# Gate and up products with both parts of the activations in one matmul of 512 columns

## The chip, the cores and the metric

One core of a Trainium2 chip runs one program. The metric is the device time of one execution in microseconds (us). Most executions of a kernel agree within 0.3%. The kernel must give float32 results close to those of the reference, which is why every large product is made from operands cut into two parts.

## The reference

Two blocks work on x [256 tokens, 1024 features] in float32. The first has two layers, each of a gated feed-forward block, three mixers side by side (a recurrence over 6 heads, dilated attention, a gated convolution) with an input and an output projection, and a second gated feed-forward block:

```
_swiglu(x, w_gate, w_up, w_down) = (silu(x @ w_gate) * (x @ w_up)) @ w_down
x = x + 0.5 * _swiglu(_rms_norm(x, norm_ffn1[l]), ...)
x = x + mix @ w_out[l]
x = x + 0.5 * _swiglu(_rms_norm(x, norm_ffn2[l]), ...)
```

The second block has one layer: attention, a short convolution and windowed means side by side, and a feed-forward block in which gate and up pass a convolution of three taps over the tokens before silu(gate) * up. There are thus five feed-forward blocks, each with 2816 hidden units, that is 22 hidden tiles of 128.

## The kernel before

**Layout.** Features lie on partitions and tokens along the free dimension: a tile of x is [128 features, 256 tokens], and there are 8 of them (ND). A hidden tile is [128 hidden units, 256 tokens].

**Two parts.** Every large operand a is cut into a high part (rounded to float32r) and a low part (what is left). A product is three matmuls: high by high, high by low, low by high; the product of the two low parts is left out. `piece` (line 258) loads a [128, 1024] piece of weights into a raw tile (3 of these), makes the high part on ScalarE (line 271, 6 tiles) and the low part on VectorE (line 272, 5 tiles). In the last feed-forward block the down weights are also freed of their rows' mean (lines 266 to 269). `hilo` (line 322) and `split` (line 394) make the two parts of activations, in two tiles xh and xl. `mm3` (line 278) issues the three matmuls; the weight block is the stationary operand and is loaded anew before each, the activations stream through, 256 columns. All records of matmuls stand on line 276, in `mm`.

**One feed-forward block** (`ffn`, line 414). For each of the 22 hidden tiles: three pieces (gate, up, down); 8 x 2 weight blocks of gate and up products, alternating between gate and up, into one bank of PSUM named rk, gate in its first half and up in its second (lines 427 to 431); the gate step (line 446, or line 1136 in the last block); the two parts hh and hl of the hidden tile (lines 434 to 437); then the 8 down products of the hidden tile before, into four banks that stay for the whole block (two named mm, two named at; lines 438 to 440). So a hidden tile's down products follow the gate and up products of the next one. The last three hidden tiles are kept: their down products come at the end, output tile by output tile (`ends`, line 405): for five output tiles those of the first two kept hidden tiles, then, output tile by output tile, those of the last hidden tile, each followed by the residual and the next norm.

The very first hidden tile (`fresh`) takes all gate products before the up products; its weights arrive with x.

**Gate steps.** `swiglu` multiplies both halves of the bank by the norm's factor R in one VectorE instruction (line 448), then silu on ScalarE (450) and a product on VectorE (452). `conv_gate` takes each half by a ScalarE instruction with scale and bias (line 1141) and two taps on VectorE (1142, 1143), and between hidden tiles one step of the next norm's work on the residual (lines 1073 and 1083).

**What sets the order.** The framework's scheduler puts the instructions of each engine in order by priority and by a model of their times, and gives out the tiles; each engine then works through its queue in that order. In the trace VectorE casts weight pieces between the steps of the gate. The eight banks of PSUM are named mm (3), rk (2) and at (3); `accs` (line 391) takes two mm and two at.

**Other users of the parts.** `colsB` (line 325) and `colsA` (line 332) make the input projections; in `colsA` the activations are the stationary operand and the weights stream with up to 512 columns. `w_out` (line 951) makes the output projections, `Norm.tile` (line 357) and `LayerNorm.end` (line 1098) cut x for the products that follow.

Of the kernel before, what the change touches and what calls it, by code (L numbers as in the profile page):

```python
# [21 lines left out]
FIRST = 2 * 3 * ND + 128      # of the small arrays: the gains of the norms, and the identity  # L22
# [4 lines left out]
KO = (0, 2, 4, 6, 1, 3, 5, 7)      # so that neighbours lie in different banks of PSUM  # L27
EXPH = math.exp(-0.5)
ALPHA = 2.0 ** 0.25
NEG = -1e30  # L30


# ---------------------------------------------------------------- host side: layout, and constants of the shapes
class Pack:
    """small arrays side by side in one [128, n] array"""
# [17 lines left out]
def _pt(v):  # L53
    """[n*128] -> [128, n]"""
    return v.reshape(-1, 128).T


def _ffn_pack(g, u, d):
    """[22*128, 3072]: for each tile of 128 hidden units its gate columns, up columns, down rows"""
    out = np.empty((NF, 128, 3, 1024), np.float32)  # L60
    out[:, :, 0] = g.reshape(8, 128, NF, 128).transpose(2, 1, 0, 3).reshape(NF, 128, 1024)
    out[:, :, 1] = u.reshape(8, 128, NF, 128).transpose(2, 1, 0, 3).reshape(NF, 128, 1024)
    out[:, :, 2] = d.reshape(NF, 128, 1024)
    return out.reshape(NF * 128, 3072)


def _cols(w, c0, n):
    """columns c0..c0+n of w [K, *] -> [128, K/128 * n]"""
# [99 lines left out]
# ---------------------------------------------------------------- the kernel  # L168
@with_exitstack
def tile_model(ctx, tc, A, at, out):  # L170
# [55 lines left out]
    # ---- constants  # L226
# [30 lines left out]
    # ---- weights: a piece is [128, <=1024] of a DRAM array; hi + lo is the piece exactly  # L257
    def piece(src, r0, c0, n=1024, centre=False):
        """centre: each row less its mean"""
# [18 lines left out]
    def mm3(out, ah, al, bh, bl, start, stop):  # L278
        """out += (ah + al).T @ (bh + bl), without the product of the two low parts"""
        mm(out, ah, bh, start, False)  # L280
        mm(out, ah, bl, False, False)
        mm(out, al, bh, False, stop)

    def rsqrt(v, n, tag, eng):
        """[128, n] 1/sqrt(v) to float32: a first value from the exponent, then three Newton steps"""
# [18 lines left out]
    def spread(ps, r):  # L304
        """ps [128, T] <- r [128 tokens, 2] along the free dimension, the same in every partition"""
# [3 lines left out]
    def head_rsqrt(sqs, scale, eps_, b, rb, tag, eng):  # L309
        """sqs: [128 = 2 heads x 64, T] each; rb [128 tokens, 2, 128 * len(sqs)] gets each head's factor 64 times"""  # L310
# [11 lines left out]
    def hilo():  # L322
        return (xs.tile([128, T], F32R, name="xh", bufs=10), xs.tile([128, T], F32R, name="xl", bufs=11))

    def colsB(ps, w, hl, start):
        """ps [128 columns, T] from a piece of 8 k-tiles x 128 columns"""
        hi, lo = w
        for k in KO:
            s = slice(k * 128, k * 128 + 128)
            mm3(ps, hi[:, s], lo[:, s], *hl[k], start=start and k == KO[0], stop=k == KO[-1])  # L330

    def colsA(ps, ws, n, hl, half):
        """ps [128 tokens, n] from pieces of (1024 // n) k-tiles x n columns"""
        kp = 1024 // n
        s = slice(half * 128, half * 128 + 128)
        for k in range(ND):
            hi, lo = ws[k // kp]
            c = slice((k % kp) * n, (k % kp) * n + n)
            xh, xl = hl[k]
            mm(ps, xh[:, s], hi[:, c], k == 0, False)  # L340
            mm(ps, xl[:, s], hi[:, c], False, False)
            mm(ps, xh[:, s], lo[:, c], False, k == ND - 1)

    # ---- the residual stream, features on partitions; the first weights between its parts
# [6 lines left out]
    class Norm:  # L351
        """x*g split into its two parts, and 1/rms for the products' results"""
# [4 lines left out]
        def tile(self, d):  # L357
            if not self.hl:
                self.st = bank("at")
            xh, xl = hilo()  # L360
            act.activation(xh, x[:, d], AF.Identity, scale=par(self.g, d))
            dve.scalar_tensor_tensor(xl, x[:, d], par(self.g, d), xh.bitcast(F32), op0=OP.mult, op1=OP.subtract)
# [13 lines left out]
            self.hl[d] = (xh, xl)  # L376
# [17 lines left out]
    def split(src, scale=None, to=None):  # L394
        """both parts of src * scale (a column, or a number)"""
        hi, lo = to or hilo()
# [6 lines left out]
        return hi, lo  # L403

    def ends(parts, finish):
        """the last products of each tile, tile by tile; the very last part may still be on its way"""
# [7 lines left out]
    def ffn(src, hl, gate, finish, centre=False, tail=TAIL, early=()):  # L414
# [5 lines left out]
        def down(d, i, wd, hh, hlo):  # L420
            s = slice(d * 128, d * 128 + 128)
            mm3(acc[d // 2][:, d % 2], wd[0][:, s], wd[1][:, s], hh, hlo,
                start=(i == 0 and d % 2 == 0), stop=(i == NF - 1))

        for i in range(NF):
            wg, wu, wd = [early.pop() if early else piece(src, i * 128, c * 1024, centre=centre and c == 2) for c in range(3)]
            b = bank("rk").rearrange("p (j t) -> p j t", j=2)
            ks = range(ND) if fresh else KO
            for k, j, w in [(k, j, w) for k in ks for j, w in ((0, wg), (1, wu))] if not fresh else [(k, j, w) for j, w in ((0, wg), (1, wu)) for k in ks]:
                s = slice(k * 128, k * 128 + 128)  # L430
                mm3(b[:, j], w[0][:, s], w[1][:, s], *hl[k], start=(k == ks[0] and j == 0), stop=(k == ks[-1]))
            fresh = False
            h = gate(i, b)
            hh = t1("hh", F32R)
            act.activation(hh, h, AF.Copy)  # L435
            hlo = t1("hl", F32R)
            dve.tensor_sub(hlo, h, hh.bitcast(F32))
# [4 lines left out]
            wait.append((i, wd, hh, hlo))  # L442
# [20 lines left out]
    # ---- attention over heads: exp(-(score + bias) * scale' - max), normalised while it is transposed  # L463
    def attend(h, q, k, vtok, bias_of, scale, o=None):
        """one head; the second of a pair takes the first's bank and gives both heads' parts"""
# [30 lines left out]
    def relative_bias():  # L496
        """[128, 8, T] of 8 * rel_bias[h, bucket(128 + p - t)] to DRAM, the future at NEG (8x: scores come unscaled)"""
# [23 lines left out]
    # ---- the three mixers of the first block  # L521
    rel = []

    def mixers(l, hl, R, rtok):
# [14 lines left out]
        def shifted(tiles, dst):  # L539
            """R * products, then each token mixed with the one before"""  # L540
# [16 lines left out]
        def head_rsqrt_qk(sqs, rb):  # L557
            """q and k come without the token's 1/rms r: r / sqrt(r^2 m + eps) for each head"""
# [610 lines left out]
```

## Time and profile before

| | |
|---|---|
| Time, median of 3 runs | 1488.86 us (1487.58 to 1492.49) |
| Profiled execution, from first to last instruction | 1489.3 us (its time is given by this span alone) |
| TensorE, mean granted clock | 0.981 of full speed |
| TensorE matmuls | 12034 |
| Weight loads (PEld) | 12034, busy 1388.8 us |
| DMA | 231.36 MB, mean 155 GB/s |
| Loads of weight pieces for the feed-forward blocks | 330, of 512 KB each |

Times are us unless marked ns. PE is the matmul side of TensorE and PEld its weight loads, which overlap matmuls; DVE is VectorE, ACT ScalarE, POOL GpSimd. A row names line, engine, operation and output<-inputs by the program's names. Matmuls are pipelined, so the records of matmuls that follow each other overlap; how fast they go is read from their starts. "Idle before" is the time in which the engine had nothing to do before the instruction, and the name behind the arrow is what released it. In the timeline the first two figures are start and duration.

### The profile page before, as it was taken

The page shows a single profiled execution, that of the slowest core. Times are in us where ns is not written, and L with a number is a line of the kernel's source. Part 1 is how long each engine was busy: PE and PEld are TensorE (multiplying, and loading weights), DVE is VectorE, ACT ScalarE, POOL GpSimd, SP SyncE. Part 2 cuts the span into 40 slices and gives each one's busy share as a digit, 9 for nine tenths or more (in the row PEclk, how much of TensorE's full clock was granted, in tenths as well). Part 3 has the DMA queues.
Part 4 walks back from the last instruction along what each step waited for, and adds up shares of the span by engine and source line. Part 5 has one row for each costly group of instructions (what it writes and reads, how often), then busy time and mean ns, then how long its engine had stood idle before and what let it go on. Part 6 is the DMA issues. An engine that isn't in the chain of part 4 may idle for free.

```text
span 1489.3 us, 29165 instructions
## 1 busy us (share of the span) xinstructions
PE 1447.8 (97%) x12034; PEld 1388.8 (93%) x12034; DVE 937.6 (63%) x1719; ACT 791.1 (53%) x1335; POOL 29.7 (2%) x98
## 2 busy tenths in 40 slices
PE   7999999899999999999999989999999999899997
PEld 6999999877999999999999977899999988899997
DVE  6555577765755556555556966665555645677775
ACT  5444456363544445444447454454444566777675
POOL 1000000200000000000000010000000000000000
PEclk9999999989999999999999988999999999999998
DMA  7655554330455655555554421255655652465561
GB/s 256 190 186 173 186 169 127 114 112 12 147 177 186 191 176 158 182 185 185 183 179 141 121 75 57 89 164 178 189 185 173 193 158 87 123 195 174 188 186 63
DMA packets 67526, 231.36 MB, mean 155 GB/s; under 512 B 7449, under 2 KB 11329, under 8 KB 67393
## 3 DMA queue, kind: packets, MB, share of 16 engines
q1 hardware_dynamic: 67392, 229.50, 49.6%
q8 instruction: 94, 1.54, 0.4%
q14 instruction: 40, 0.32, 0.1%
HBM read 227.37 MB, written 2.11 MB: 154 GB/s over the span
## 4 chain that ended last, share of the span: by engine, by line
PE 81%; issue 14%; DVE 1%; ACT 1%; POOL 1%; DMA 1%; SPq 0%; POOLq 0%; ACTq 0%; DVEq 0%
PE rk L276 41%; PE mm L276 24%; PE at L276 16%; DVE lo L272 1%; DMA raw<-ffn 0%; DMA raw<-win 0%; ACT x L1111 0%; POOL nt L291 0%; POOL nt L295 0%; ACT hi L271 0%; PE mm L815 0%; PE mm L809 0%; POOL nt L290 0%; SPq L347 0%; ACT P L477 0%
## 5 line engine op out<-in xcount | busy, mean ns | idle before, releaser
L272 DVE TENSOR_TENSOR lo<-raw,hi 128x1024 fp32r<-128x1024 f32 (+1 forms) x392 | 476.1, 1216 | 360.1 <-PE rk L276 298.9
L271 ACT ACTIVATE hi<-raw 128x1024 fp32r<-128x1024 f32 (+1 forms) x392 | 407.2, 1052 | 390.0 <-PE rk L276 199.9
L276 PE MATMUL rk<-xh,hi 128*128 128x256 f32 x1792 | 509.1, 285 | 11.8 <-ACT hi L271 10.3
L276 PE MATMUL rk<-xh,lo 128*128 128x256 f32 x1792 | 510.2, 285 | 1.9 <-DVE lo L272 1.9
L276 PE MATMUL rk<-xl,hi 128*128 128x256 f32 x1792 | 508.6, 284 | 0.0
L276 PEld LDWEIGHTS rk<-xh,hi 128*128 128x128 f32 x1792 | 345.0, 193 | 12.1 <-ACT hi L271 10.3
L276 PEld LDWEIGHTS rk<-xh,lo 128*128 128x128 f32 x1792 | 345.0, 193 | 3.7 <-DVE lo L272 3.0
L276 PEld LDWEIGHTS rk<-xl,hi 128*128 128x128 f32 x1792 | 345.2, 193 | 0.1
L276 PE MATMUL mm<-xl,hi 128*128 128x256 f32 x496 | 143.1, 289 | 0.1
L276 PE MATMUL mm<-xh,lo 128*128 128x256 f32 x496 | 143.2, 289 | 0.0
L276 PE MATMUL mm<-xh,hi 128*128 128x256 f32 x496 | 141.4, 286 | 0.0
L276 PE MATMUL at<-hh,hi 128*128 128x256 f32 x440 | 124.4, 284 | 0.0
L276 PE MATMUL at<-hl,hi 128*128 128x256 f32 x440 | 124.3, 283 | 0.0
L276 PE MATMUL at<-hh,lo 128*128 128x256 f32 x440 | 124.3, 283 | 0.0
L276 PE MATMUL mm<-hl,hi 128*128 128x256 f32 x440 | 124.3, 284 | 0.0
L276 PE MATMUL mm<-hh,lo 128*128 128x256 f32 x440 | 124.1, 283 | 0.0
L276 PE MATMUL mm<-hh,hi 128*128 128x256 f32 x440 | 123.9, 285 | 0.0
L276 PEld LDWEIGHTS mm<-xl,hi 128*128 128x128 f32 x496 | 95.6, 193 | 2.3 <-issue 1.8
L276 PEld LDWEIGHTS mm<-xh,lo 128*128 128x128 f32 x496 | 95.5, 193 | 2.0 <-issue 1.5
L276 PEld LDWEIGHTS mm<-xh,hi 128*128 128x128 f32 x496 | 95.4, 193 | 0.7 <-ACT v L1006 0.3
L435 ACT ACTIVATE hh<-h 128x256 fp32r<-128x256 f32 x110 | 45.8, 417 | 83.9 <-DVE h L452 77.4
L276 PEld LDWEIGHTS mm<-hl,hi 128*128 128x128 f32 x440 | 84.4, 192 | 0.2
(328 smaller groups left out, 2059.8 us busy)
## 6 DMA issues: line engine op xcount, KB each, us to landing
raw<-ffn SPq DMA_DIRECT2D x330, 512.0 KB, 4.3
raw<-win SPq DMA_DIRECT2D x60, 512.0 KB, 4.0
raw<-wout SPq DMA_DIRECT2D x24, 512.0 KB, 3.7
raw<-win SPq DMA_DIRECT2D x8, 384.0 KB, 3.3
bias<-dbias SPq DMA_DIRECT2D x12, 128.0 KB, 2.0
x<-x SPq DMA_DIRECT2D x4, 256.0 KB, 3.6
rows<-ebd SPq DMA_DIRECT2D x4, 256.0 KB, 5.3
rel<-relo SPq DMA_DIRECT2D x4, 256.0 KB, 3.5
```

Source lines behind the costliest of these rows:

```text
L271: act.activation(hi[:, :n], raw[:, :n], AF.Copy)
L272: dve.tensor_sub(lo[:, :n], raw[:, :n], hi[:, :n].bitcast(F32))
L276: pe.matmul(out, lhsT, rhs, start=start, stop=stop, skip_group_check=True)
L435: act.activation(hh, h, AF.Copy)
```

## The change

The two parts of an activation tile now lie in one tile [128, 2, 256]. In `ffn` a new helper takes the place of `mm3` for gate and up: the low weights meet the high activations in a matmul of 256 columns, and the high weights meet both parts in one of 512. Gate and up have a bank each: the first half takes high by high, the second half the two corrections. ScalarE copies the second half out, VectorE adds the first half to it, and the gate step reads the sum from SBUF. Hidden tiles take their two banks in turn from the two rk, and from one mm and one at. The down products and all others stay with three matmuls. In `colsA` the second and third matmul change places. Comments are dropped throughout. The core of the diff:

```diff
-    def mm3(out, ah, al, bh, bl, start, stop):
-        mm(out, ah, bh, start, False)
-        mm(out, ah, bl, False, False)
-        mm(out, al, bh, False, stop)
+    def mm3(out, ah, al, b, start, stop):
+        mm(out, ah, b[:, 0], start, False)
+        mm(out, ah, b[:, 1], False, False)
+        mm(out, al, b[:, 0], False, stop)
+
+    def mm2(out, ah, al, b, start, stop):
+        mm(out[:, 1], al, b[:, 0], start, False)
+        mm(out, ah, b, False, stop)
...
     def hilo():
-        return (xs.tile([128, T], F32R, name="xh", bufs=10), xs.tile([128, T], F32R, name="xl", bufs=11))
+        return xs.tile([128, 2, T], F32R, name="xhl", bufs=11)
...
-            xh, xl = hl[k]
-            mm(ps, xh[:, s], hi[:, c], k == 0, False)
-            mm(ps, xl[:, s], hi[:, c], False, False)
-            mm(ps, xh[:, s], lo[:, c], False, k == ND - 1)
+            mm(ps, hl[k][:, 0, s], hi[:, c], k == 0, False)
+            mm(ps, hl[k][:, 0, s], lo[:, c], False, False)
+            mm(ps, hl[k][:, 1, s], hi[:, c], False, k == ND - 1)
...
         for i in range(NF):
...
-            b = bank("rk").rearrange("p (j t) -> p j t", j=2)
+            b = [bank(t).rearrange("p (j t) -> p j t", j=2) for t in (("rk", "rk"), ("mm", "at"))[i % 2]]
...
-                mm3(b[:, j], w[0][:, s], w[1][:, s], *hl[k], start=(k == ks[0] and j == 0), stop=(k == ks[-1]))
+                mm2(b[j], w[0][:, s], w[1][:, s], hl[k], start=(k == ks[0]), stop=(k == ks[-1]))
             fresh = False
-            h = gate(i, b)
-            hh = t1("hh", F32R)
-            act.activation(hh, h, AF.Copy)
-            hlo = t1("hl", F32R)
-            dve.tensor_sub(hlo, h, hh.bitcast(F32))
+            q = t3("q")[:, :512].rearrange("p (j t) -> p j t", j=2)
+            for j in range(2):
+                act.activation(q[:, j], b[j][:, 1], AF.Copy)
+                dve.tensor_tensor(q[:, j], b[j][:, 0], q[:, j], op=OP.add)
+            h = gate(i, q)
+            h2 = tmp.tile([128, 2, T], F32R, name="h2", bufs=3)
+            split(h, to=h2)
...
-            wait.append((i, wd, hh, hlo))
+            wait.append((i, wd, h2))
```

The same joined tiles are passed through `Norm.tile`, `split`, `pair`, `LayerNorm.end`, the mixers and `w_out`, with no other change there.

## Rows read from the trace of the kernel before

**Rows 1.** The page: busy us (share of the span) xinstructions, by engine.

```profile
PE 1447.8 (97%) x12034; PEld 1388.8 (93%) x12034; DVE 937.6 (63%) x1719; ACT 791.1 (53%) x1335; POOL 29.7 (2%) x98
```

**Rows 2.** The page: the chain that ended last, shares by engine.

```profile
PE 81%; issue 14%; DVE 1%; ACT 1%; POOL 1%; DMA 1%; SPq 0%; POOLq 0%; ACTq 0%; DVEq 0%
```

**Rows 3.** Busy time by stretch: each engine's us, TensorE's granted clock, DMA share, GB/s.

```profile
44.88:191.90 147.02, 147.02 (x1226) 146.88 (x1225) 81.26 (x103) 66.96 (x87) 0.00 (x0) 1.00 0.58 183
1310.00:1462.00 152.00, 152.00 (x1268) 151.95 (x1267) 113.03 (x174) 109.30 (x177) 0.00 (x0) 1.00 0.59 181
```

**Rows 4.** Groups of instructions by form: us busy, mean ns | idle time before, releasers.

```profile
L276 PE MATMUL rk<-xh,hi 128*128 128x256 f32 x1792 | 509.1, 285 | 11.8 <-ACT hi L271 10.3 <-ACT xh L1117 1.5
```

**Rows 5.** Timeline of TensorE, start and us: 24, then 48 matmuls apart.

```profile
68.36 0.28 PE L276 MATMUL mm<-hh,hi 128*128 128x256 f32 x1
...
71.25 0.28 PE L276 MATMUL rk<-xh,hi 128*128 128x256 f32 x1
...
77.00 0.28 PE L276 MATMUL mm<-hh,hi 128*128 128x256 f32 x1
```

**Rows 6.** Timeline of TensorE: matmuls of 512 columns, 24 apart.

```profile
1194.56 0.39 PE L276 MATMUL mm<-hi,xh 128*128 128x512 f32 x1
...
1200.00 0.39 PE L276 MATMUL mm<-hi,xh 128*128 128x512 f32 x1
```

**Rows 7.** Groups by form: a copy out of PSUM, an addition with PSUM, SwiGLU steps.

```profile
L452 DVE TENSOR_TENSOR h<-gu,s 128x256 f32<-128x256 f32 x88 | 36.9, 420 | 5.1 <-ACT s L450 5.1
L450 ACT ACTIVATE s<-gu 128x256 f32<-128x256 f32 x88 | 36.3, 413 | 2.8 <-DVE gu L448 2.7
...
L398 ACT ACTIVATE xh<-at 128x256 fp32r<-128x256 f32 x10 | 3.8, 385 | 11.0 <-PE at L276 11.0
...
L1090 DVE TENSOR_TENSOR x<-x,mm 128x256 f32<-128x256 f32 x8 | 3.2, 421 | 4.5 <-PE mm L276 4.5
```

**Rows 8.** Groups of VectorE that started before 69.5 us.

```profile
L272 DVE TENSOR_TENSOR lo<-raw,hi 128x1024 fp32r<-128x1024 f32 x23 | 28.1, 1223 | 19.7 <-PE rk L276 7.7 <-ACT hi L271 6.5 <-issue 5.5
L448 DVE TENSOR_TENSOR gu<-rk,R 128x512 f32<-128x512 f32 x7 | 4.8, 684 | 0.0
```

**Rows 9.** Timeline of VectorE in one steady hidden tile.

```profile
68.26 1.23 DVE L272 TENSOR_TENSOR lo<-raw,hi 128x1024 fp32r<-128x1024 f32 x1 [3.87 <-PE rk L276]
69.41 0.68 DVE L448 TENSOR_TENSOR gu<-rk,R 128x512 f32<-128x512 f32 x1
...
72.61 0.42 DVE L437 TENSOR_TENSOR hl<-h,hh 128x256 fp32r<-128x256 f32 x1
```

**Rows 10.** Timeline, all engines, at the end of the first feed-forward block.

```profile
195.75 0.28 PE L276 MATMUL mm<-hh,hi 128*128 128x256 f32 x1
...
199.37 0.42 DVE L437 TENSOR_TENSOR hl<-h,hh 128x256 fp32r<-128x256 f32 x1 [0.48 <-ACT hh L435]
...
199.85 0.39 PE L276 MATMUL mm<-hl,hi 128*128 128x256 f32 x1
```

**Rows 11.** Timeline of VectorE and ScalarE, one hidden tile of the last block.

```profile
1357.57 1.23 DVE L272 TENSOR_TENSOR lo<-raw,hi 128x1024 fp32r<-128x1024 f32 x1 [1.07 <-PE rk L276]
1359.12 1.28 DVE L269 SCALAR_TENSOR_TENSOR lo<-raw,wmean,hi 128x1024 fp32r<-128x1024 f32 x1 [0.33 <-ACT hi L268]
1360.32 0.47 DVE L1142 SCALAR_TENSOR_TENSOR gu<-rk,pk,gu 128x255 f32<-128x255 f32 x1
...
1361.35 0.56 ACT L1141 ACTIVATE gu<-rk,pk 128x256 f32<-128x256 f32 x1 [0.86 <-DVE gu L1143]
...
1364.38 0.43 DVE L437 TENSOR_TENSOR hl<-h,hh 128x256 fp32r<-128x256 f32 x1 [0.49 <-ACT hh L435]
```

**Rows 12.** Timeline of TensorE at the start.

```profile
11.52 0.58 PE L276 MATMUL rk<-xh,lo 128*128 128x256 f32 x1 [0.47 <-DVE lo L272]
11.90 0.41 PE L276 MATMUL rk<-xh,hi 128*128 128x256 f32 x1
12.11 0.41 PE L276 MATMUL rk<-xl,hi 128*128 128x256 f32 x1
```

More of the change, by code (lines that the diff above doesn't have):

```diff
@@ L329, in colsB @@
             s = slice(k * 128, k * 128 + 128)
-            mm3(ps, hi[:, s], lo[:, s], *hl[k], start=start and k == KO[0], stop=k == KO[-1])
+            mm3(ps, hi[:, s], lo[:, s], hl[k], start=start and k == KO[0], stop=k == KO[-1])
     def colsA(ps, ws, n, hl, half):
@@ L359, in tile @@
                 self.st = bank("at")
-            xh, xl = hilo()
-            act.activation(xh, x[:, d], AF.Identity, scale=par(self.g, d))
-            dve.scalar_tensor_tensor(xl, x[:, d], par(self.g, d), xh.bitcast(F32), op0=OP.mult, op1=OP.subtract)
+            xhl = hilo()
+            act.activation(xhl[:, 0], x[:, d], AF.Identity, scale=par(self.g, d))
+            dve.scalar_tensor_tensor(xhl[:, 1], x[:, d], par(self.g, d), xhl[:, 0].bitcast(F32), op0=OP.mult, op1=OP.subtract)
             sq = t1("sq")
@@ L375, in tile @@
             self.sq = sq
-            self.hl[d] = (xh, xl)
+            self.hl[d] = xhl
         def end(self):
@@ L394, in split @@
     def split(src, scale=None, to=None):
-        hi, lo = to or hilo()
+        hl = hilo() if to is None else to
+        hi, lo = hl[:, 0], hl[:, 1]
         if scale is None:
@@ L402, in split @@
             dve.scalar_tensor_tensor(lo, src, scale, hi.bitcast(F32), op0=OP.mult, op1=OP.subtract)
-        return hi, lo
+        return hl
     def ends(parts, finish):
@@ L418, in ffn, with down @@
         fresh = bool(early)
-        def down(d, i, wd, hh, hlo):
+        def down(d, i, wd, h2):
             s = slice(d * 128, d * 128 + 128)
-            mm3(acc[d // 2][:, d % 2], wd[0][:, s], wd[1][:, s], hh, hlo,
+            mm3(acc[d // 2][:, d % 2], wd[0][:, s], wd[1][:, s], h2,
                 start=(i == 0 and d % 2 == 0), stop=(i == NF - 1))
@@ L799, in mixers @@
                 s = slice(c * 128, c * 128 + 128)
-                mm(b[:, :384], hl[k][0][:, s], hi[:, cc], k == 0, False)
-                mm(b[:, :384], hl[k][1][:, s], hi[:, cc], False, False)
-                mm(b[:, :384], hl[k][0][:, s], lo[:, cc], False, k == ND - 1)
+                mm(b[:, :384], hl[k][:, 0, s], hi[:, cc], k == 0, False)
+                mm(b[:, :384], hl[k][:, 0, s], lo[:, cc], False, False)
+                mm(b[:, :384], hl[k][:, 1, s], hi[:, cc], False, k == ND - 1)
             act.activation(va[:, c], b[:, :384], AF.Identity, scale=rtok[:, c:c + 1])
@@ L956, in part @@
             s = slice(d * 128, d * 128 + 128)
-            mm3(acc[d // 2][:, d % 2], ws[i][0][:, s], ws[i][1][:, s], *mix[order[i]],
+            mm3(acc[d // 2][:, d % 2], ws[i][0][:, s], ws[i][1][:, s], mix[order[i]],
                 start=(i == 0 and d % 2 == 0), stop=(i == 7))
@@ L1009, in pair @@
     def pair():
-        t = u3("mx", F32R)
-        return t[:, :T], t[:, T:2 * T]
+        return u3("mx", F32R)[:, :2 * T].rearrange("p (j t) -> p j t", j=2)
     for f in range(4):
@@ L1115, in end @@
                 else:
-                    xh, xl = hilo()
-                    act.activation(xh, x[:, d], AF.Identity, bias=par(self.n + "_b", d))
-                    dve.scalar_tensor_tensor(xl, x[:, d], par(self.n + "_b", d), xh.bitcast(F32), op0=OP.add, op1=OP.subtract)
-                    hl[d] = (xh, xl)
+                    hl[d] = hilo()
+                    act.activation(hl[d][:, 0], x[:, d], AF.Identity, bias=par(self.n + "_b", d))
+                    dve.scalar_tensor_tensor(hl[d][:, 1], x[:, d], par(self.n + "_b", d), hl[d][:, 0].bitcast(F32), op0=OP.add, op1=OP.subtract)
             if not last:
```

## The prediction

> **What bounds the kernel now.** I read the views in this order: the busy times of the page, its chain of work that ended last, the busy times by stretch, the groups of instructions, and then the timeline, engine by engine, in one steady hidden tile, at an end and in the last feed-forward block. The busy times show TensorE at 97% of the span and VectorE at 63%, ScalarE at 53% [rows 1]; the chain that ended last lies on TensorE for 81%, and "issue", time between its own instructions, is 14% [rows 2]. An average hides stages, so the next thing to see is the steady part: in 147 us of the first feed-forward block and in 152 us of the last one TensorE has no idle time at all, at full granted clock [rows 3]. There, whatever TensorE no longer has to do comes off the time, as long as VectorE and ScalarE keep up.
>
> The products that the change rewrites are the three groups of 1792 matmuls that write rk; the other two have the same count as the one shown [rows 4]. Of each 1792, 32 belong to other products (the small lora columns: 2 layers of 8, and a quarter of the last output projection: 4 inputs by 4 tiles), which leaves 1760 = 5 blocks of 22 hidden tiles x 16 weight blocks.
>
> What one of them costs is not its duration of 285 ns, since matmuls overlap; it is the distance from start to start. From the first down product at 68.36 to the next gate product at 71.25 lie 24 matmuls, to the next down product at 77.00 another 48: 8.64 us over 72, **120.0 ns** for 256 columns [rows 5]. The kernel already has matmuls of 512 columns with a new weight block before each: 24 of them take 5.44 us, **226.7 ns** each [rows 6]. [...]
>
> **The change, part by part.** *Two matmuls for three.* The columns streamed per weight block stay 768. Before: 3 x 120.0 = 360.0 ns. After: 120.0 + 226.7 = 346.7 ns. That is 13.3 ns a block, 1760 x 13.3 = **-23.5 us**, and a steady hidden tile goes from 8.64 to 8.43 us. No row alternates 256 with 512 columns, so the 346.7 is an estimate. Its ends are nothing saved (the wide one costs two narrow ones) and 23.5; I take 23.5, because the 512-column row is the same operation on operands of the same type, with a fresh weight block each time.
>
> [...]
>
> *Bringing the two halves together.* New per hidden tile: two ScalarE copies of 256 columns out of PSUM (nearest row 385 ns) and two VectorE additions with one operand in PSUM (421 ns) [rows 7]. Over 110 hidden tiles that is 85 us more on ScalarE and 93 us more on VectorE, about 59% and 70% of the new span: neither engine becomes the bound by its sum. What counts is whether TensorE ever waits for what they do. Three places:
>
> (a) *Weights of the next tile.* Both engines cut each weight piece into high and low part in queue order. At 68.26, when 23 low parts and 7 gate steps have been started by 69.5 [rows 8], the 23rd is the up weights' low part of the next tile; it starts as the gate products end and before the gate step [rows 9]. It ends at 69.49, 1.1 us after the down products start (call that start E), and TensorE now wants it in the first matmul of the second weight block, at E + 24 x 0.120 + 0.347 = E + 3.23. The cover is 2.1 us. Even with both additions (0.84) in front of it, it is in time: cost 0. It costs something from the point where it starts after E + 2.0.
>
> (b) *The hidden tile itself.* Its low part ends at 72.61 + 0.42 = 73.03, E + 4.7 [rows 9], and the down products that read it start at E + 8.64 (77.00), after the change E + 8.43. A copy and two additions make it at most E + 5.9: 2.5 us of cover are left, cost 0. The two banks that a hidden tile now takes (one before) come free earlier than now: the copy and the addition read them and need no factor of the norm. Behind the copies on ScalarE's queue stand the high-part casts of later pieces; two copies hold them up by 0.8 us at most, the low parts after them and the next loads into the raw tiles as well, and the DMA engines are busy for 0.58 of the stretch [rows 3]: cost 0.
>
> (c) *The ends.* After the last tile only 30 products (3.6 us) stand before the first that reads it. In the first block they start at 195.75; its low part is ready at 199.37 + 0.42 = 199.79, and the matmul that reads it starts at 199.85 [rows 10]. There is no cover: each delay is paid. The copy lies beside the weight cast that VectorE is doing; the two additions, 0.84 us, are added to the chain. Five blocks: **+4.2 us**. Ends: 0, if a weight cast of 1.22 us that stands inside this chain is put elsewhere, and 5 x (0.84 + 1.22) = 10.3, if one more slips in. I take the middle, because nothing in the trace moves a cast either way.
>
> *The last block* has the most work beside the matmuls. VectorE per hidden tile: casts 2 x 1.23 + 1.28, four taps of 0.47, three steps of 0.43 (h, its low part, one on the residual), 6.9 us [rows 11]. With 0.84 more it is 7.75 of 8.43 us: still under TensorE, cost 0. The other end: of its waits now, 0.49 and 0.33 us [rows 11] are inside the chain; if they stay and the copy's 0.385 is added as a third, 7.75 + 1.2 = 8.95, 0.52 us over, 22 x 0.52 = 11 us. Zero is nearer, since ScalarE's wait of 0.86 us for VectorE, which reads the same PSUM bank [rows 11], goes: both read SBUF now. The sum of tokens in this block needs a bank that odd tiles now use: once, 0 to 2 us; I take 0.
>
> *The start.* The first matmul used the high part alone; now the low part comes first. Of the first block two matmuls stand ahead of the one that waits for the low part until 11.52; matmuls lie 0.21 us apart there (11.90, 12.11) [rows 12]. These two now run after 11.52: **+0.4 us** (0 to 2, if the first casts hold TensorE up). Joined tiles for the two parts of x, the reordered token products and the freed small tiles cost nothing: same counts, widths and casts.
>
> **Sum.** -23.5 + 4.2 + 0.4 = -18.9 us against the profiled 1489.3, 1470.4; the median of the runs is 0.4 below that span, so **1470.0**.
>
> **Rivals.**
> - *The last block is held by VectorE* (the 11 us above): 1481. For it: only 0.7 us of VectorE a tile are left. Against: the bank wait that goes. Chance 0.10.
> - *Slower: the low part of the up weights comes late.* Place: VectorE's queue at E. If the whole gate chain is put ahead of that cast, it starts after copy 0.385, additions 0.84, gate step 0.68, ScalarE's 0.41 and the product's 0.42 [rows 7, 9], at E + 2.74, ends at E + 3.97, and TensorE waits 0.74 us in each of 88 tiles: 65 us, 1535. It decides from a start after E + 2.0. Against it: the cast stands first in this trace [rows 9]. Chance 0.05.
> - *The wide matmul is not one:* the operand of two parts is issued as two of 256, or costs 240 ns. Nothing is saved, the 4.6 us stay: 1493.5, slower. Against: [rows 6]. Chance 0.05.
> - *Little of the 13.3 ns goes with the instruction:* if a fifth does, 2.7 ns x 1760 = 4.7 us, eaten by the 4.6: 1488.8, no change. [...] Chance 0.05. [...]
>
> **How the numbers follow.** The forecast has 0.75. Its own range is 1465 (no cost at the ends) to 1477 (one more cast at each end, the first casts late). A measurement here tells about 0.3%, 4.5 us, from no change. Faster: 0.75 + 0.10 = 0.85; same 0.05; slower 0.05 + 0.05 = 0.10. The range takes in the first rival and a microsecond of spread below: 1464 to 1482.
>
> **What would show it.** Right: 1760 TensorE matmuls fewer (12034 to about 10274); in the new profile starts that alternate 0.120 and 0.227 us; 8.43 us from one tile's down products to the next; no idle time in the steady stretches; some tenths of waiting for the hidden tile at the five ends. Wrong: matmuls that wait for a low part in the steady part (second rival), a period above 8.43 in the last block only (first), a pitch sum of 0.360 with fewer or as many matmuls (third, fourth).

## The result and the profile after

| | before | after |
|---|---|---|
| Time, median of four runs each | 1489.41 us (1487.58 to 1492.49) | 1524.3 us (1504.86 to 1546.52) |
| Ratio to the kernel before | | 1.0121, 95% interval 1.0072 to 1.0171 |
| Profiled execution, from first to last instruction | 1489.3 us | 1511.5 us (its time: 1513.35) |
| TensorE, mean granted clock there | 0.981 | 0.963 |

In the median the changed kernel is slower, by 2.3% here and by 1.4% when it was measured again (after_again below). The ratios in this document leave out executions that are over 1.5% above the fastest of their kernel, 8 of all 14 of the changed kernel, so the medians of all executions stand beside them.

The page of the kernel after, busy times, TensorE's row of the 40 slices, its granted clock, and the chain that ended last ([rows 1, 2] of before):

```profile
PE 1463.0 (97%) x10274; PEld 1314.6 (87%) x10274; DVE 1028.6 (68%) x1939; ACT 841.3 (56%) x1555; POOL 29.5 (2%) x98
...
PE   6999999989999999999999999999999999899997
...
PEclk9999999965999999999999996999999999999999
...
PE 79%; issue 14%; DVE 3%; ACT 2%; DMA 1%; POOL 1%; POOLq 0%; SPq 0%; ACTq 0%
```

1760 matmuls are gone, as predicted, VectorE is at 68% and ScalarE at 56%. TensorE is as busy as before, 97% of a longer span. The clock row says where to look: in the ninth and tenth slice it is granted 0.6 and 0.5. The steady stretches ([rows 3]) of the first and of the last feed-forward block:

```profile
48.00:185.00 137.00, 137.00 (x904) 124.94 (x903) 91.66 (x129) 70.76 (x114) 0.00 (x0) 1.00 0.62 187
1330.00:1450.00 120.00, 115.50 (x748) 103.28 (x747) 94.20 (x162) 89.02 (x164) 0.00 (x0) 1.00 0.57 177
```

The first has no idle time, the last has 4.5 us of 120. TensorE's timeline in one steady hidden tile, first down product, first and second weight block, first down product of the next tile ([rows 5]):

```profile
77.32 0.40 PE L276 MATMUL mm<-h,hi 128*128 128x256 f32 x2
...
80.16 0.28 PE L276 MATMUL rk<-xhl,lo 128*128 128x256 f32 x1
80.28 0.39 PE L276 MATMUL rk<-xhl,hi 128*128 128x512 f32 x1
80.51 0.28 PE L276 MATMUL rk<-xhl,lo 128*128 128x256 f32 x1
...
85.81 0.40 PE L276 MATMUL mm<-h,hi 128*128 128x256 f32 x2
```

From 80.16 to 85.81 lie 16 weight blocks: 5.65 us, **353.1 ns** each, where 360.0 were spent and 346.7 predicted. From 77.32 to 80.16 lie 24 down products: 118.3 ns each, 120.0 before. The tile takes 8.49 us, down from 8.64; 8.43 were predicted.

To see where the time went, the profiled executions are cut at the gate steps' products (h<-gu), first and last of each block. Three of the runs of the next section stand beside before and after, and the best version (both_grp4):

| Stage, us | before | after | hold | before_push | last_only | both_grp4 |
|---|---|---|---|---|---|---|
| start to the first hidden tile | 22.6 | 25.4 | 25.8 | 23.4 | 23.4 | 25.9 |
| four SwiGLU blocks, 21 periods each | 693.4 | 681.3 | 681.5 | 693.9 | 690.7 | 678.5 |
| mixers of layer 0 | 212.8 | **238.2** | 212.8 | 231.3 | 210.0 | 212.6 |
| mixers of layer 1 | 209.3 | 211.5 | 215.5 | 217.4 | 203.4 | 210.3 |
| between the layers | 22.4 | 21.9 | 21.9 | 22.3 | 22.3 | 22.0 |
| mixing of the second block | 137.1 | 134.2 | 134.3 | 136.1 | 134.9 | 136.2 |
| last feed-forward block, 21 periods | 174.1 | **180.8** | 179.3 | 174.1 | 178.6 | 169.7 |
| end | 17.6 | 18.2 | 19.0 | 17.9 | 18.8 | 17.6 |

After against before: -12.1 in the SwiGLU blocks, -2.9 in the second block's mixing, and against that +25.4 in the mixers of layer 0, +6.7 in the last block, +2.8 at the start, +2.2 in layer 1: +22.2 us in all.

**The last block.** Waits of all engines in 1310 to 1470 us after: us in total, times, longest.

```profile
ACT raw L266 <- DMA raw<-ffn: 20.5, 16, 2.4
DVE h L405 <- ACT h L404: 13.2, 7, 3.5
DVE q L442 <- ACT q L441: 11.1, 8, 2.0
...
PEld mm L276 <- ACT h L404: 4.5, 5, 1.8
```

ScalarE waits 20.5 us for loads of weights at line 266, the pass that sums the rows of the down weights. In its queue the copies of the corrections come behind such a pass (ScalarE's timeline after):

```profile
1408.00 1.06 ACT L266 ACTIVATE raw<-raw 128x1024 f32<-128x1024 f32 x1 [2.38 <-DMA raw<-ffn]
...
1409.06 0.64 ACT L441 ACTIVATE q<-rk 128x256 f32<-128x256 f32 x2
```

and the wait goes on to VectorE's addition (11.1 us), to the hidden tile and to TensorE.

**The mixers of layer 0.** Beside the joined tiles, nothing was changed there but the order of two matmuls in the token products of 384 columns: 48 of them per layer, which make v for the dilated attention. No count changed. The same two stretches of before and after, 16 us in which the recurrence's triangular solve runs on tiny matmuls, and the 58 us behind it (columns as in [rows 3]):

```profile
297.00:313.00 16.00, 14.05 (x212) 9.91 (x211) 10.91 (x25) 9.40 (x21) 2.21 (x3) 0.79 0.56 172
313.00:371.00 58.00, 55.79 (x402) 42.95 (x402) 33.29 (x98) 29.27 (x80) 0.15 (x1) 0.97 0.11 36
```

```profile
297.00:313.00 16.00, 11.28 (x340) 7.32 (x340) 12.78 (x33) 9.42 (x20) 2.21 (x3) 1.00 0.52 170
313.00:371.00 58.00, 55.89 (x243) 44.21 (x245) 22.27 (x57) 19.81 (x54) 0.15 (x1) 0.50 0.12 35
```

After (the second fence), TensorE is busy for 55.89 of 58 us as before, but at half clock (0.50 granted) all the time, and gets through 243 matmuls where it got through 402. What it did ahead of that differs too. Groups of TensorE in 297 to 313 us, before and then after:

```profile
L276 PE MATMUL mm<-lo,xh 128*128 128x384 f32 x8 | 3.2, 403 | 0.0
L276 PE MATMUL mm<-hi,xl 128*128 128x384 f32 x7 | 2.7, 393 | 0.0
L276 PE MATMUL mm<-hi,xh 128*128 128x384 f32 x7 | 2.7, 388 | 0.0
```

```profile
L276 PE MATMUL mm<-hi,xhl 128*128 128x384 f32 x1 | 0.4, 447 | 0.0
```

Before, the solve's own products run from 293.65 to 308.48 us; 23 of the 48 token products lie ahead of them, 11 between its steps and 14 right behind the last step. After, 47 lie ahead, one between and none behind, and TensorE has 11.28 us of work in 16; two waits for a load of rows are 2.8 us of the rest. The last product of the solve before and the first token product behind it, then the first of the solve after and the last token product:

```profile
308.47 0.20 PE L276 MATMUL rk<-Y32b,A 32*32 32x32 f32 x2
308.60 0.44 PE L276 MATMUL mm<-hi,xl 128*128 128x384 f32 x1
```

```profile
296.94 0.98 PE L276 MATMUL rk<-X,XM 32*32 32x16 f32 x96
297.85 0.45 PE L276 MATMUL mm<-hi,xhl 128*128 128x384 f32 x1
```

The scheduler orders each engine's queue for the whole program, and the changed blocks changed what it did with stages that the edit hardly touches.

### The profile page after: what moved, and what is told of

Its sections match the earlier page's. It is cut to its first block, busy times and chain, and to the rows that moved or that the text cites. A ratio compares the mean times of both kernels' runs of the same rounds, so it can differ in the third digit from the quotient of the medians.

```text
span 1511.5 us, 26049 instructions
## 1 busy us (share of the span) xinstructions
PE 1463.0 (97%) x10274; PEld 1314.6 (87%) x10274; DVE 1028.6 (68%) x1939; ACT 841.3 (56%) x1555; POOL 29.5 (2%) x98
## 4 chain that ended last, share of the span: by engine, by line
PE 79%; issue 14%; DVE 3%; ACT 2%; DMA 1%; POOL 1%; POOLq 0%; SPq 0%; ACTq 0%
PE mm L276 31%; PE at L276 24%; PE rk L276 23%; DVE lo L272 1%; DMA rows<-ebd 1%; ACT hi L271 0%; DMA raw<-ffn 0%; DMA x<-x 0%; DVE q L442 0%; POOL nt L300 0%; ACT x L1118 0%; POOL ny L301 0%; DVE gu L456 0%; DVE xhl L367 0%; DVE ca L599 0%
## 5 line engine op out<-in xcount | busy, mean ns | idle before, releaser
L271 ACT ACTIVATE hi<-raw 128x1024 fp32r<-128x1024 f32 (+1 forms) x392 | 411.1, 1052 | 134.3 <-DMA raw<-ffn 77.2
L276 PE MATMUL mm<-xhl,hi 128*128 128x256 f32 (+1 forms) x1432 | 367.0, 324 | 0.4 <-DVE xhl L405 0.4
L276 PE MATMUL rk<-xhl,hi 128*128 128x512 f32 (+1 forms) x944 | 330.9, 394 | 0.0
L276 PE MATMUL rk<-xhl,lo 128*128 128x256 f32 x912 | 259.2, 285 | 15.9 <-DVE lo L272 14.3
L276 PE MATMUL mm<-xhl,lo 128*128 128x256 f32 x936 | 268.1, 287 | 0.0
L276 PEld LDWEIGHTS mm<-xhl,hi 128*128 128x128 f32 x1432 | 242.8, 194 | 22.5 <-issue 3.6
L276 PEld LDWEIGHTS rk<-xhl,hi 128*128 128x128 f32 x944 | 177.4, 190 | 37.2
L276 PE MATMUL at<-xhl,hi 128*128 128x512 f32 (+1 forms) x568 | 198.2, 373 | 0.0
L276 PEld LDWEIGHTS rk<-xhl,lo 128*128 128x128 f32 x912 | 174.2, 191 | 17.7 <-DVE lo L272 15.3
L276 PEld LDWEIGHTS mm<-xhl,lo 128*128 128x128 f32 x936 | 180.7, 193 | 1.0 <-issue 0.3
L276 PE MATMUL mm<-h,hi 128*128 128x256 f32 x880 | 167.3, 284 | 4.4 <-ACT h L404 3.4
```

The lines of the kernel that those rows point to most:

```text
L271: act.activation(hi[:, :n], raw[:, :n], AF.Copy)
L276: pe.matmul(out, lhsT, rhs, start=start, stop=stop, skip_group_check=True)
```

## The experiments

Theory 1: the new order of the mixers leaves TensorE too little to do in the solve, its clock falls, and the work behind runs at half clock. (That the order costs the clock, and why it does, are two claims; the runs show the first.) Rivals: the new form of the products draws the clock down by itself; the joined tiles cost something; it was chance. For the last block: the copies in ScalarE's queue (theory A), or the banks and matmuls (B).

**The changed kernel again** (after_again, no edit).

> The changed kernel once more, for the spread of its time and a second profile. Theory 1 (the order of the mixers of layer 0 costs TensorE its clock): 1500 to 1515 us, with a stretch at half clock of about 58 us beginning near 313 us, and about 25 us more than before between the two hidden stages of layer 0. Rival (that stretch was chance in one execution): 1480 to 1490 us in most executions, and no such stretch in this profile.

Median 1510.18 us of ten (1486.38 to 1529.14), where 25 executions of the kernel before beside it have 1489.67; ratio 1.0015 (0.9985 to 1.0045). Its profile has the stretch of 58.0 us at half clock again, from 311.8 us, and 236.0 us for the mixers. But four of the ten ended at 1486 to 1499 us, with mean clocks of 0.969 to 0.980: the program makes the fall likely, it doesn't force it. At like clock it is a little faster than before: 1486.38 us at 0.980, where 14 executions of the kernel before at 0.980 took 1488.93 to 1493.97.

**Token products held behind the solve** (hold).

```diff
         for c in range(2):
             b = bank()
+            if c and l == 0:
+                mm(b[qs[0], 0:32], A32[qs[1], 0], Y32[qs[1], 0])
             for k in range(ND):
```

> The changed kernel, but in layer 0 the second half of the 48 token products (24 of 384 columns) is held behind the triangular solve, by one tiny product written first into their bank. Theory 1: the stretch of about 58 us at half clock is gone or down to under 20 us, and the time falls by 20 to 27 us to 1480 to 1490 us. Rival 1 (the two-matmul form in the feed-forward block draws the clock down, whatever the mixers' order): the half clock stays, 1500 to 1515 us. Rival 2 (chance): no difference from the changed kernel run beside it.

The tiny product ties the second half (24) of the token products to a late step of the solve. In the trace 24 run ahead of the solve (292.91 to 304.95 us), none between its steps and 24 right behind it. The same stretches as above:

```profile
297.00:313.00 16.00, 14.49 (x166) 9.43 (x166) 11.16 (x25) 11.87 (x26) 2.21 (x3) 0.84 0.36 124
313.00:371.00 58.00, 56.62 (x414) 43.96 (x414) 31.98 (x100) 26.77 (x77) 0.15 (x1) 0.94 0.13 42
```

The clock is back, 414 matmuls fit, and the mixers of layer 0 take 212.8 us, as before the change. The median is 1496.75 us (1491.71 to 1505.07 of ten), 13 us under after_again on the same chip and not the 20 to 27 of theory 1, and still over the kernel before (ratio 1.0053, 1.0028 to 1.0077). The two profiled executions are 19.5 us apart; the medians are nearer, since four of after_again's ten ended at 1486 to 1499 us without the cure. Layer 1 still lost its clock for 27.3 us from 882.3 us, as after the change (27.3 us from 903.8).

**The same order without the change** (before_push).

```diff
+        va_ = c3("va"); va = va_[:, :768].rearrange("p (c n) -> p c n", c=2)
+        ws = [piece(W, 0, 20 * 1024 + i * 768, 768) for i in range(4)]
+        for c in range(2):
...
         X32, Y32 = half("X32", 12), half("Y32", 12)
...
-        va_ = c3("va"); va = va_[:, :768].rearrange("p (c n) -> p c n", c=2)
-        ws = [piece(W, 0, 20 * 1024 + i * 768, 768) for i in range(4)]
-        for c in range(2):
```

> The kernel before, its feed-forward blocks untouched, but the 48 token products are written ahead of the solve, and so run ahead of it as they do in the changed kernel. Theory 1: a half-clock stretch of 40 to 60 us follows the solve of layer 0 and the time rises by 15 to 28 us to 1504 to 1517 us. Rival 1 (the feed-forward form draws the clock down): no such stretch, 1486 to 1493 us.

```profile
297.00:313.00 16.00, 14.70 (x291) 10.05 (x293) 12.09 (x30) 9.55 (x21) 2.21 (x3) 0.69 0.59 190
313.00:371.00 58.00, 57.09 (x328) 44.62 (x320) 22.44 (x63) 20.36 (x58) 0.15 (x1) 0.55 0.05 17
```

1513.78 us, ratio 1.015 (1.0109 to 1.0191), all four executions at 0.958 to 0.969. Half clock begins at 303.2 us and lasts 61.4; the busy time in the first row is in part that of slower matmuls. The mixers of layer 0 take 231.3 us and those of layer 1, whose token products the edit moves as well, 217.4. The old products with the new order lose what the change lost: the order is enough, and rival 1 is not needed.

**Joined tiles alone** (layout_only): three matmuls into one bank again, no copies, no additions.

```diff
-            b = [bank(t).rearrange("p (j t) -> p j t", j=2) for t in (("rk", "rk"), ("mm", "at"))[i % 2]]
+            b = bank("rk").rearrange("p (j t) -> p j t", j=2)
...
-                mm2(b[j], w[0][:, s], w[1][:, s], hl[k], start=(k == ks[0]), stop=(k == ks[-1]))
+                mm3(b[:, j], w[0][:, s], w[1][:, s], hl[k], start=(k == ks[0] and j == 0), stop=(k == ks[-1]))
```

> The changed kernel with joined tiles for the two parts of x, but gate and up again as three matmuls into one bank, without the copies and additions. All theories that put the loss on the order or on the two-matmul form: as the kernel before, 1486 to 1492 us, and the 48 token products spread over the solve as before. Rival 3 (the joined tiles themselves cost something, by coarser waits): 1495 to 1515 us.

1483.61 us, ratio 0.9966 (0.9938 to 0.9993): a little faster than either, and than the 1486 to 1492 expected, so joined tiles cost nothing. In its trace 11 token products lie between the solve's steps again and 14 behind it, as before (at 291, 296, 303 and 305 us, each behind tiny products), although the tiles are joined and the token products reordered; so it is the two-matmul form in the SwiGLU blocks, with its copies, additions and banks, that makes the scheduler change them. Which of these does it was not tried.

**The form in the last block alone** (last_only): the two-matmul form where `centre` is set, three elsewhere.

> Two matmuls per block in the last feed-forward block alone, three in the four SwiGLU blocks; the token products then lie among the solve's steps as in the kernel before, without any hold. Theory (the form costs the last block its ScalarE queue, and nothing else): its 21 periods take 179 to 181 us in place of 174, the mean clock stays at 0.978 to 0.986, the median is 1486 to 1496 us. Rival (the two-matmul form itself draws the clock down): under 0.975 in most executions, over 1500 us.

The token products lie between the solve's steps here too (292, 296, 303 and 306 us). 1490.34 us, ratio 1.0005 (0.9982 to 1.0029); mean clock 0.976 to 0.986 in all ten executions, mixers 210.0 and 203.4 us, the last block 178.6, just under the 179 expected. In the last block the form leaves the clock alone and costs 4.5 us. As this block comes behind all mixers, the run can't say what the form in the SwiGLU blocks does to the mixers; hold does, and q_dve_last and both_grp4 below: they have the form in those blocks, and no stretch of 27 us or more at half clock in layer 0.

**The last block without the extra work** (no_q_last; hold with)

```diff
+            if centre:
+                h = gate(i, [b[0][:, 0], b[1][:, 0]])
+            else:
...
```

> The kernel of the run hold, but in the last feed-forward block the gate reads the first half of each bank alone: the copies of the correction halves and their additions (ScalarE 44 x 0.37, VectorE 44 x 0.42 us) are left out there, and with them the correction from the low parts in that block. The matmuls stay. Theory A (this work on ScalarE and VectorE delays the hidden tiles of the last block): its 21 periods fall from 179.3 to 170 to 172 us. Theory B (the two banks of a tile, or the matmuls themselves, delay it): they stay at 177 to 180 us.

169.3 us: theory A. (1467.04 us in the median of two, at a clock of 0.987.)

**The copies on VectorE** (q_dve_last; hold with)

```diff
             for j in range(2):
-                act.activation(q[:, j], b[j][:, 1], AF.Copy)
+                if centre:
+                    dve.tensor_copy(q[:, j], b[j][:, 1])
+                else:
+                    act.activation(q[:, j], b[j][:, 1], AF.Copy)
```

> The kernel of the run hold, but in the last feed-forward block the copies of the correction halves are made by VectorE in place of ScalarE; the sum of the work on both engines is about the same. Theory A1 (the copies stand in ScalarE's queue behind a pass over weights that still waits for its DMA): the last block's 21 periods fall from 179.3 to 171 to 175 us. Theory A2 (VectorE's load, 144 of 170 us here, is what delays the tiles, and 44 x 0.4 us more of it makes it the bound): they rise to 182 to 190 us.

170.8 us, with all of the work there: theory A1. The block in that profile, and the waits that are left on ScalarE at line 266:

```profile
1310.00:1470.00 160.00, 159.80 (x1042) 144.60 (x1041) 141.65 (x259) 116.55 (x188) 0.00 (x0) 1.00 0.61 181
```

```profile
ACT raw L266 <- DMA raw<-ffn: 7.1, 6, 2.5
```

VectorE is now busy for 141.65 of 160 us, and TensorE hardly waits (159.80). So the sum of the work was never too much; what hurt was its place behind an instruction that waits for a DMA. Nor is it ScalarE as such: in grp16_hold below, where the widths are in another order, the copies stay on ScalarE and the block takes 170.6 us, with little waiting at line 266. The whole block in hold, then in grp16_hold:

```profile
ACT raw L266 <- DMA raw<-ffn: 22.9, 18, 2.4
```

```profile
ACT raw L266 <- DMA raw<-ffn: 6.4, 8, 1.5
```

Of 40 copies in each block (the 20 inner hidden tiles), 8 in hold follow a pass of line 266 directly, and one in grp16_hold. The wait alone costs nothing: no_q_last has 25.6 us of it, with no copies behind it, and its block takes 169.3 us. A copy behind such a pass starts when the pass is over: in after one starts at 1400.34 us, at the end of a pass that had waited 1.57 us for its load (1399.29 + 1.06), though the last product into the bank that it reads started at 1397.25 and took 0.40; VectorE's addition waited 2.01 us for it. The whole: 1486.88 us, ratio 0.995 (0.9908 to 0.9993), at clocks of 0.968 to 0.984.

**Three matmuls in the last block** (hold_last_old; hold with `mm3` where `centre` is set).

> The kernel of the run hold, but with three matmuls per block in the last feed-forward block, as before the change. The last block's 21 periods: 173.5 to 174.5 us, and the median 5 to 7 us under that of hold, 1489 to 1492 us, if that block's loss is its own; unchanged if it comes from the state that the kernel arrives in.

173.5 us in the block, as expected, but a median of 1495.45 us (ratio 1.0002, 0.9964 to 1.004): in the profile the mixers of layer 0 took 227.3 us, with half clock for 27.3 us from 315.3 us, despite the held products. At a mean clock of 0.966 it took 1498.98 us, where hold, on another chip, took 1503.76 and 1505.07: 5 to 6 us less at like clock, which is about the block's part (179.3 less 173.5).

**Another order of the widths** (grp16_hold): first all 16 matmuls of 512 columns of a hidden tile, then the 16 of 256.

```diff
-                mm2(b[j], w[0][:, s], w[1][:, s], hl[k], start=(k == ks[0]), stop=(k == ks[-1]))
+            for part in range(2):
+                for j, k, w in [(j, k, w) for k in ks for j, w in ((0, wg), (1, wu))]:
...
+                    if part == 0:
+                        mm(b[j], w[0][:, s], hl[k], k == ks[0], False)
+                    else:
+                        mm(b[j][:, 1], w[1][:, s], hl[k][:, 0], False, k == ks[-1])
```

> The kernel of the run hold, with the same matmuls of a hidden tile in another order: first the 16 of 512 columns, then the 16 of 256. Theory W (each change of width costs: 117.3 + 236.0 ns for a pair, where neighbours of one width start 120.0 and, in the product of 512 columns, 226.7 ns apart): 346 to 348 ns per block in the mean, 5 to 6 ns less, so hidden tiles of 8.40 to 8.43 us in place of 8.49 and 5 to 8 us less in the four SwiGLU blocks. Rival (the cost is the second bank half written again at once, or the pace of 353.3 ns is the engine's for this work): 8.47 to 8.50 us.

Both came true at once. Neighbours of one width start 228.1 and 119.5 ns apart in the mean (44 to 190 us), 347.6 a block; but hidden tiles take about 9.6 us, and the whole 1570.46 us (ratio 1.0523, 1.0443 to 1.0602). Waits in 60 to 190 us:

```profile
DVE q L446 <- ACT q L445: 49.7, 14, 3.8
...
PEld mm L276 <- ACT h L404: 10.1, 14, 1.0
PE mm L276 <- ACT h L404: 7.0, 12, 0.8
```

VectorE waits up to 3.8 us for the copies, and the hidden tile is late for its down products in nearly every tile.

**Idle filled with other work** (fill): the changed kernel's order, and products that nobody reads tied to three steps of layer 0's solve, such as

```diff
         act.activation(A16, b, AF.Identity, scale=m1)
+        if l == 0:
+            fb = bank("at")
+            mm(fb[qs[0], 0:16], Y32[qs[0], 0], A16[qs[0], 0])
+            for _ in range(2):
+                mm(fb, ones, x[:, 0:2])
```

> The changed kernel with the 48 token products of layer 0 where the change put them, ahead of the solve, but six products of 512 columns whose results nobody reads are put between the steps of that solve (two behind each of three steps, each two tied to their step by a tiny product), so that TensorE works on while the steps of the solve wait for VectorE and ScalarE. Theory 1a (the clock falls because TensorE has too little to do in the solve, whatever it is that it does): the stretch of about 58 us at half clock falls under 25 us and the mixers of layer 0 take 212 to 224 us in place of 236 to 238, although work is added. Rival 1b (it is the place of the token products, by buffers or waits, and the clock only goes along): the half clock stays and the mixers take 236 to 246 us.

Neither fits well. The stretch at 313 us is gone, but another of 37.5 us begins at 343.2, and the mixers take 231.5 us. The ten executions lie between 1477.43 us at a clock of 0.989 and 1518.16 at 0.960 (median 1503.65, ratio 1.0004, 0.9966 to 1.0041): one execution kept its clock with the added work, above any of the 14 without it (0.980 at most), and most did not.

**Both cures, and pairs of equal width.** both: hold without `and l == 0`, and the copies of q_dve_last. grp4: q_dve_last with this order; both_grp4 (and both_grp4_again, the same kernel) has all three:

```diff
-                mm2(b[j], w[0][:, s], w[1][:, s], hl[k], start=(k == ks[0]), stop=(k == ks[-1]))
+                for j, w in ((0, wg), (1, wu)):
+                    mm(b[j][:, 1], w[1][:, s], hl[k][:, 0], k == ks[0], False)
+                for j, w in ((0, wg), (1, wu)):
+                    mm(b[j], w[0][:, s], hl[k], False, k == ks[-1])
```

> The changed kernel with both cures: token products held behind the solve in both layers, and the copies of the last block made by VectorE. Theory 1 also for layer 1: its time at half clock (30.7 us in the profile of hold) falls under 15 us, its mixers take 200 to 208 us in place of 211 to 222, and the whole 1470 to 1480 us. Rival (layer 1 falls to half clock in the dependent small products behind the solve, which no order of the token products feeds): 10 to 45 us at half clock as before, and 1476 to 1495 us.

> The kernel of the run q_dve_last (token products held in layer 0, last block's copies on VectorE) with the four matmuls of one pair of weight blocks in the order 256, 256, 512, 512 columns. Theory W (a change of width costs): 120.0 + 117.3 + 226.7 + 236.0 = 700 ns for two blocks in place of 706.6, hidden tiles of 8.44 us in place of 8.49, each SwiGLU block's 21 periods 168.3 to 168.8 us in place of 169.5, and 4 to 6 us less in the whole at equal clock. Rival (the order makes the hidden tiles late, as the full grouping did): over 170 us.

> All three: token products held in both layers, copies of the last block on VectorE, and pairs of equal width. If each cure holds: 1465 to 1476 us, under the kernel before by 13 to 24 us. If layer 1 still loses its clock: 1475 to 1492 us.

> The best version again, for its spread: the median 1472 to 1478 us, ratio 0.988 to 0.994, clock 0.980 to 0.986 in nearly all executions. If the four executions seen were lucky: some under 0.970 and over 1490 us, as both had one of eleven.

| | median us (n) | ratio to before, 95% | mean clock |
|---|---|---|---|
| both | 1479.63 (11) | 0.9933, 0.991 to 0.9955 | 0.968 to 0.986 |
| grp4 | 1496.17 (7) | 1.0016, 0.997 to 1.0062 | 0.949 to 0.982 |
| both_grp4 | 1474.87 (4) | 0.9911, 0.9889 to 0.9933 | 0.982 to 0.985 |
| both_grp4_again | 1474.68 (6) | 0.9887, 0.986 to 0.9914 | 0.981 to 0.985 |

both differs from q_dve_last by the hold in layer 1 alone, and ten of its eleven executions have clocks of 0.976 or more; in its profile layer 1 is at half clock for 17.1 us, a little over the 15 of theory 1, and its mixers take 207.8. The eleventh execution, which was the profiled one, had 54.6 us at half clock in layer 0 with the products held, so the order shifts the odds there too and no more. grp4 misses in the whole (held in layer 0 only, clocks down to 0.949; in its profile both layers lost their clock, layer 0 for 30.7 us at a stretch), but its SwiGLU blocks fit theory W: 21 periods of the second block in 168.5 us for 169.5, a tile in 8.45 us. both_grp4 beats both kernels, by about 1% against the one before, in two measurements on two chips. Part of its gain may be luck in the clock: none of its ten executions fell, and both, with the same holds, fell once in eleven. Its stretches:

```profile
297.00:313.00 16.00, 14.37 (x172) 9.53 (x171) 11.53 (x29) 12.84 (x28) 2.21 (x3) 0.87 0.36 119
313.00:371.00 58.00, 56.86 (x419) 44.35 (x419) 33.95 (x106) 25.92 (x75) 0.15 (x1) 1.00 0.13 41
```

Over all profiles, a stretch of 27 us or more at half clock in layer 0 goes with the place of the token products. Of four profiles with 47 or 48 of them ahead of the solve (after, after_again, before_push, fill) all have it; of three that have them ahead, between and behind (before, layout_only, last_only) none; of nine with half of them held behind the solve, three (hold_last_old, both, grp4). In the held ones none lies between the steps, so the runs don't show that filling the solve's gaps is what keeps the clock: bulk work right behind the solve goes with it as well.

## Why the prediction was wrong

1470.0 us (1464 to 1482) and 0.85 for faster were predicted; the median was 1524.3 us. By the prediction's own steps:

- *What bounds it* was right: TensorE, at 97% before and after, with no idle time in the steady SwiGLU tiles.
- *"Two matmuls for three", -23.5 us* was right in its sign and too large. 353.1 ns instead of 346.7: 6.9 ns a block were saved, half of the 13.3. The prediction took both widths from rows in which neighbours have one width [rows 5, 6]; where they alternate, 256 to 512 takes 117.3 ns and 512 to 256 takes 236.0. grp16_hold shows the difference: 347.6 ns with the same matmuls grouped. The four SwiGLU blocks gave 12.1 us, of which 2.6 are the joined tiles' (layout_only takes 690.8 us), so the form gave 9.5; by the prediction's figure 4 x 352 x 13.3 ns = 18.7 would have come.
- *(a) Weights of the next tile* and *(b) the hidden tile, cost 0* were right in the SwiGLU blocks: 137.00 of 137 us busy. The second rival didn't happen.
- *(c) The ends, +4.2* came out at the low end that the prediction gave. At the end of the first block two matmuls start 0.36 us apart (198.03, 198.39) where 0.12 is the pace, some 0.2 us of waiting in place of 0.84: the weight cast that stood inside the chain now runs ahead of the additions. The stage between the layers, which holds one such end, went from 22.4 to 21.9 us. *The start, +0.4* was +2.8, over its own bound of 2; it is 24.5 to 26.1 us in every run with the form in the first block, and no run says why.
- *The last block, cost 0* was wrong. The first rival gave it 11 us at 22 x 0.52; against the 171 us that the SwiGLU blocks' pace would give, it cost some 10. But the rival's mechanism, VectorE's load, is not what runs show: with still more on VectorE the block fell to 170.8 us (q_dve_last). The place in ScalarE's queue was the cause, and the prediction's step (b) had looked at what stands behind the copies there, and not at what stands in front.
- *The step that failed* is one sentence of the part on the start: "the reordered token products ... cost nothing: same counts, widths and casts". It priced the stages outside the feed-forward blocks by their instructions. The order that it speaks of, that of two matmuls among the token products, did cost nothing: layout_only has it too. But their place among the solve's products changed, and with it the clock. By the clock records of the two traces, half clock in the inner stages (all but start and end) grew from 47.8 us before to 105.8 after; half of the difference, 29.0 us, is an estimate of what full clock would have saved, against +27.6 in the mixers of both layers. before_push made the loss without the change, and hold, in its profile, has the change without the loss of layer 0. No rival had this mechanism.

What stays open is why the clock stays down for so long. From 313 to 371 us TensorE is recorded busy for 55.89 of 58 us, and yet half clock is granted throughout; by the mean clocks (0.936 to 0.980 in the 14 executions), the same program can have the stretch in one execution and not in the next. fill was meant to tell whether it is the amount of work or the place of the token products, and came out between.

At like clock the sum is small and of the predicted sign: 2.6 to 7.6 us faster, by the one execution at 0.980 above. A straight line of time over mean clock through all 14 executions of the changed kernel and one through the 83 of the kernel before that were made beside the experiments give 1486.9 and 1491.8 us at 0.980, an estimate of 5 us. The 12 us of the blocks are mostly given back in the last block and at the start.

## What to carry to other kernels

Where a scheduler orders whole queues, a change to one stage can reorder another: compare the order of every engine in all stages before calling the rest unchanged, and look at the granted clock by stage. Bulk matmuls between or right behind the steps of a chain of tiny ones can be worth more than their own time (mixers of layer 0: 212.8 us before, 238.2 after); a dependency can hold them there if the scheduler would take them away. Here that raised the odds of a full clock, and didn't secure it: with the products ahead of the solve four of four profiles had 27 us or more at half clock at a stretch in layer 0, otherwise three of twelve. Before an instruction is added to a queue, look at what may stand in front of it and wait: moving the copies away from there took the last block from 179.3 us (hold) to 170.8 (q_dve_last).

## What the runs showed of the hardware

- The distance between starts of matmuls with fresh weights depends on the order of the widths. In groups of one width (grp16_hold), 256 then 256 takes 119.5 ns and 512 then 512 takes 228.1, together 347.6. Where they alternate (after), 256 then 512 takes 117.3 and 512 then 256 takes 236.0, together 353.3. In pairs of equal width (both_grp4) two blocks take 115.4 + 115.5 + 232.9 + 233.7 = 697.5 ns, 348.8 each. The next matmul's width alone doesn't settle it: 512 then 512 is 228.1 in one order and 232.9 in the other.
- With both parts of an operand in one tile the old three matmuls went slightly faster: a steady tile of 8.61 us in layout_only for 8.64, by its down products (118.9 ns for 120.0; 118.3 after). Nothing in the runs says why.
- Half clock lasted up to 64.9 us at a stretch (grp4, from 895.6 us, in layer 1) while TensorE was recorded busy for 63.63 of them.
